# A two-layer trunk: the modulation pieces of FFN two and three computed in the Even mixer, each visit's matmuls in reversed order

## The chip, the cores and the metric

The kernel runs on one core of one Trainium2 chip. Its time is device microseconds of one execution. The core's engines run side by side and wait for each other by semaphores: TensorE (PE; PEld is its weight load), VectorE (DVE), ScalarE (ACT), GpSimd (POOL) and SyncE (SP), which here only issues DMAs. ACT issues some DMAs as well.

## The reference

640 tokens of width 1024 (128 context tokens, 512 latent ones) pass two layers. Each layer is an FFN half step, a token mixer and another FFN half step, each between two RMS norms and each modulated by a condition (one vector for the context tokens, one for the latent ones):

```python
def adaln(cond, w, b):                       # mod_w[i]: 1024 x 9216, one per layer
    m = (silu(cond) @ w + b).reshape(cond.shape[0], 1, 9, D_MODEL)
    return [m[:, :, j] for j in range(9)]    # shift, scale, gate for each of the three sublayers
x = x + 0.5 * gate * rmsnorm(swiglu(rmsnorm(x, g_pre) * (1 + scale) + shift), g_post)   # FFN
x = x + gate * rmsnorm(mixer(rmsnorm(x, g_pre) * (1 + scale) + shift), g_post)          # mixer
```

The mixer of layer 0 ("Even") is a bidirectional gated DeltaNet with four heads beside multi-head latent attention with four heads; that of layer 1 ("Odd") is gated linear attention. The FFN's inner width is 2816. Everything is float32.

The modulation product is the part that the change moves: 2 rows times a 1024 x 9216 matrix, twice, some 75 MB of weights for very little arithmetic.

## The kernel before

There are six sublayers in a row: FFN 1, Even, FFN 2 (layer 0), FFN 3, Odd, FFN 4 (layer 1). Large products are done as three products of float32r halves (`hi`, `lo`): `L650` is an FFN's input product, `L298` every output product, `L208` a mixer's input product. Weights go by SP's queue from HBM into seven buffers of 512 KB (`rawp`, `raw()`), are split by ACT and DVE, and the buffer is free again.

**Modulation.** `adaln` (a generator, L364 and on) works in 80 *pieces*: layer, column group q (five of 2048 columns, the last of 1024) and row block kc (eight of 128 rows). A piece loads two halves of 512 KB (one in the last group) into `raw` buffers. Every second piece there is a *visit*: the matmuls of two pieces, each 128x32 weights (the two conditions, padded to 32) against 128x512 of the matrix; the four of a piece lie at column offsets 0, 32, 64 and 96 of PE and write four stripes of one PSUM bank. A matmul shows as two records in the trace. In the first group each piece is a visit of its own. After the eighth piece of a group its result is added to a bias in one more `raw` buffer (`mb`, L403), and for four of the five groups transposed on PE (L407) in a bank of the pool `ps_pt`, of which there are two; the DVE then copies shift and scale out. Gates go to DRAM.

`filler` does one piece. It is called 8 times at the start, after each of 16 steps of FFN 1's loop and 6 times in its tail, in the mixer through `fill` 31 times (after values and z blocks, between the heads of the attention by the table `MFILL`), 10 times in FFN 2's loop and 6 in its tail, and in FFN 3's loop until nothing is left (3 pieces). `FILLS` holds the counts of FFN 1 to 4. In the mixer `look` is set: a piece's load is issued one call ahead.

**The Even mixer.** Blocks of the input product, a short convolution, then the DeltaNet in two pairs of heads: `gdn_prep`, `gdn_inverse`, `gdn_levels` (two levels with transposes, then a last level of 128x64 matmuls), `gdn_chain` (four steps and one for the context, each a `gdn_step`), with the attention heads `mla_head` between and beside them. The two PSUM banks of `ps_pt` and the two of `ps_dn` serve both pairs for the whole stretch (`banks`), so a modulation transpose finds no bank of `ps_pt` before they are done. At the end come `out_rows` and `finish`, which is also the seam to the next sublayer.

**What sets the order.** A scheduler orders each engine's instructions when the program is built. It walks along in time; whenever an engine is free, it takes the instruction of highest priority among those that are ready by its own estimates (program order, but for those under `ahead`). A modulation matmul that is ready can so be pulled far forward into a hole, and a visit can be cut by other work. Its estimate for a modulation matmul charges the one at column offset 0 with the whole stream of 512 columns and those at other offsets with almost nothing. In the built program, of the matmuls of the mixer from piece 43 on, 19 of 20 at offset 0 are followed by other work, and of those at offsets 32 and 64 two of 40. On the chip each engine then works strictly in that order.

Of the kernel before, what the change touches and what calls it, by code (L numbers as in the profile page):

```python
# [22 lines left out]
KC = 8  # L23
# [4 lines left out]
HW = (6400, 4096)  # L28
HT = TOK // 2
PLAIN = 2  # L30
FILLS = (((16, 6), (10, 6)), ((18, 0), (0, 0)))
EARLY = 5
SLOTS = ((2, 3, 4, 5, 6), (0, 1, 2, 3, 4))
TW = 648
# [47 lines left out]
class Trunk:  # L82
# [281 lines left out]
    def adaln(self, mod_w, mod_b, norm_post):  # L364


        nc = self.nc
        order = iter([(l, q, kc) for l in range(2) for q in range(5) for kc in range(KC)])
        ready = []

        def load():
            for l, q, kc in order:
                wt = []
                for half in range(2 if q < 4 else 1):
                    w = self.W(name="mw") if (l, q) == (0, 0) else self.raw("mw")
                    nc.sync.dma_start(w, mod_w[l, kc * P:(kc + 1) * P, q * 2048 + half * 1024:q * 2048 + half * 1024 + 1024])
                    wt.append(w)
                ready.append(wt)
                return

        for l in range(2):
            for q in range(5):
                nj = 4 if q < 4 else 2
                rows = 32 * nj
                ps = self.ps_ad.tile([P, 512], F32, tag="ad", name=self.u("ad"))
                held = []
                for kc in range(KC):
                    if not ready:
                        load()
                    held.append((kc, ready.pop(0)))  # L390
                    if self.look:
                        load()
                    one = (l, q) == (0, 0)
                    for k, wt, j in [(k, wt, j) for k, wt in held for j in range(nj)] if one or kc % 2 else []:
                        nc.tensor.matmul(ps[32 * j:32 * j + 32, :], lhsT=self.cT[:, k], rhs=wt[j // 2][:, (j % 2) * 512:(j % 2) * 512 + 512], start=k == 0, stop=k == KC - 1, tile_position=(0, 32 * j))
                    if one or kc % 2:
                        held = []
                    if kc < KC - 1:
                        yield False
                mb = self.raw("mb")  # L400
                b = mod_b[l, q * 2048:q * 2048 + 512 * nj]
                nc.scalar.dma_start(mb[0:rows, 0:512], bass.AP(b.tensor, b.offset, [[512, nj], [0, 32], [1, 512]]))
                nc.vector.tensor_add(mb[0:rows, 0:512], mb[0:rows, 0:512], ps[0:rows, :])  # L403
                if q < 4:
                    pt = self.pt()
                    for c4 in range(4):
                        nc.tensor.transpose(pt[:, c4 * P:(c4 + 1) * P], mb[:, c4 * P:(c4 + 1) * P], self.ident)  # L407
                for mi in range(nj // 2):
                    n = 2 * q + mi
                    if n % 3 < 2:  # L410
                        for r in range(2):
                            src = pt.rearrange("p (c m j r) -> p c m j r", c=4, m=2, j=2)[:, :, mi, :, r]
                            nc.vector.tensor_copy(self.modF[l][:, n, r].rearrange("p (j c) -> p c j", c=4), src)
                    else:
                        o = 64 * mi
                        g = norm_post[l, n // 3]
                        nc.scalar.dma_start(mb[o:o + 64, 512:1024], bass.AP(g.tensor, g.offset, [[512, 2], [0, 32], [1, 512]]))
                        nc.vector.scalar_tensor_tensor(mb[o:o + 64, 0:512], mb[o:o + 64, 0:512], 1.0 if n // 3 == 1 else 0.5, mb[o:o + 64, 512:1024], ALU.mult, ALU.mult)
                        for j in range(2):
                            nc.scalar.dma_start(self.gate_dr[l][n // 3][:, j * 512:j * 512 + 512], mb[o + 32 * j:o + 32 * j + 2, 0:512])  # L420
                yield True
# [471 lines left out]
class Even(Mixer):  # L893
# [87 lines left out]
    def run(self, nxt):  # L981
        T, nc, i = self.T, self.T.nc, self.i
# [3 lines left out]
        k, q, vtok, vpad = ([None] * NH for _ in range(4))  # L986
# [179 lines left out]
        def gdn_prep(pair, st, misc, ering):  # L1166
            for c in range(NT):
                cs = slice(c * P, (c + 1) * P)
                pb, pk, E = misc(), misc(), ering()
                for u, d, h in units(pair):  # L1170
                    nc.tensor.transpose(un(pb, u), gc[:, d, c, h:h + 1].to_broadcast([P, P]), T.ident)
                for h2 in range(2):
                    kc = k[2 * pair + h2][:, cs]
                    nc.tensor.matmul(un(pk, 2 * h2), lhsT=kc, rhs=kc, start=True, stop=True)
                    nc.tensor.matmul(un(pk, 2 * h2 + 1), lhsT=kc, rhs=q[2 * pair + h2][:, cs], start=True, stop=True)
                for u, d, h in units(pair):
                    nc.vector.scalar_tensor_tensor(un(E, u), un(pb, u), gc[:, d, c, h:h + 1], neg[d], ALU.subtract, ALU.min)
                nc.scalar.activation(E[:, :512], E[:, :512], AF.Exp)
                pair_view = lambda t, h2: t[:, h2 * 256:h2 * 256 + 256].rearrange("p (d t) -> p d t", d=2)
                if c:  # L1180
                    Qe = st.Q[c]
                    nc.scalar.activation(Qe, pb, AF.Exp)
                    for h2 in range(2):
                        w = pair_view(Qe, h2)
                        nc.vector.tensor_mul(w, w, q[2 * pair + h2][:, cs].unsqueeze(1).to_broadcast([P, 2, P]))
                for h2 in range(2):
                    nc.vector.tensor_mul(pair_view(st.att[c], h2), pair_view(E, h2), un(pk, 2 * h2 + 1).unsqueeze(1).to_broadcast([P, 2, P]))
                for u, d, h in units(pair):
                    nc.vector.scalar_tensor_tensor(un(st.A[c], u), un(pk, 2 * (u // 2)), nbp[:, c, d * 4 + h:d * 4 + h + 1], un(E, u), ALU.mult, ALU.mult)
# [35 lines left out]
        def gdn_levels(st):  # L1225
            for lv in (4, 5):
                mask = T.cm[:, lv].unsqueeze(1).to_broadcast([P, 4, P])
                for c in range(NT):
                    a, uu, dd = st.A[c], st.U[c], st.D[c]
                    py, pz = misc(), misc()  # L1230
                    for u in range(4):
                        nc.tensor.matmul(un(py, u), lhsT=un(a, u), rhs=un(dd, u), start=True, stop=True)
                    Y = ering()
                    nc.scalar.copy(Y[:, :512], py)
                    for u in range(4):
                        nc.tensor.matmul(un(pz, u), lhsT=un(Y, u), rhs=un(uu, u), start=True, stop=True)
                    nc.vector.copy_predicated(v4(uu), mask, v4(pz))
                    for u in range(4):
                        nc.tensor.transpose(un(py, u), un(uu, u), T.ident)
                    nc.scalar.copy(dd, py)  # L1240

            lo, hi = slice(0, 64), slice(64, 128)
            where = ((hi, lo), (lo, hi))
            for c in range(NT):
                a, uu, dd = st.A[c], st.U[c], st.D[c]
                py, pz, Y = misc(), misc(), ering()
                for u in range(4):
                    r, k = where[u % 2]
                    nc.tensor.matmul(un(py, u)[r, k], lhsT=un(a, u)[:, r], rhs=un(dd, u)[:, k], start=True, stop=True, tile_position=(0, r.start))
                by = lambda t, d: t[:, :512].rearrange("p (h d t) -> p h d t", h=2, d=2)[:, :, d]  # L1250
                for d, (r, k) in enumerate(where):
                    nc.scalar.copy(by(Y, d)[r, :, k], by(py, d)[r, :, k])
                for u in range(4):
                    r, k = where[u % 2]
                    nc.tensor.matmul(un(pz, u)[k, r], lhsT=un(Y, u)[:, k], rhs=un(uu, u)[:, r], start=True, stop=True, tile_position=(0, k.start))
                for d, (r, k) in enumerate(where):
                    nc.vector.tensor_copy(by(uu, d)[k, :, r], by(pz, d)[k, :, r])

        def gdn_step(pair, st, work, S, cu, last, ctx):

            at = lambda c: slice(c * P, (c + 1) * P)
            if not last:
                pt, kdt = misc(), work()
# [23 lines left out]
            for u, d, h in units(pair):  # L1287
                c = cu[d]
# [316 lines left out]
        one = (mb, hq, prs, pTs)  # L1605
# [486 lines left out]
```

## Time and profile before

| | |
|---|---|
| median of three runs | 2714.06 us (2709.87 to 2714.55) |
| the profiled execution | 2716.26 us, of it 2714.5 us in the span |
| mean granted clock of PE | 0.991 |
| PE busy | 2632.5 us, 97% |
| PE's weight loads | 2331.2 us, 86% |
| DVE busy | 1943.0 us, 72% |
| ACT busy | 1179.1 us, 43% |
| HBM | 113 GB/s over the span |

"Busy" is time in which at least one instruction of an engine is shown. Matmuls overlap, and their ends are modelled: the end of one can lie behind the start of the next. The granted clock is a share of 2.4 GHz; 0.50 is the lower of its two levels, 1.2 GHz.

### The profile page before, as it was taken

The numbers are of one execution on the slowest core, as the hardware profiler recorded it, in microseconds if no ns is written. First come the engines' busy times: TensorE is split into PE (matmuls) and PEld (weight loads), VectorE is DVE, ScalarE is ACT, GpSimd is POOL, SyncE is SP. The second block draws the span as 40 slices with busy tenths as digits, with TensorE's granted clock in tenths as the row PEclk, the third lists the DMA queues.
The fourth block names the chain that finished last, engine by engine and source line by source line (L and its number), as shares of the span: only waits on it lengthen the run. The fifth ranks groups of instructions, "written<-read, shape, count | busy, mean of one in ns | idle before, by whom it ended". The sixth has DMA issues, their size and how long they took to land. (4 is left out here: it accounts for less than half of the span.)

```text
span 2714.5 us, 41232 instructions
## 1 busy us (share of the span) xinstructions
PE 2632.5 (97%) x16040; PEld 2331.2 (86%) x16040; DVE 1943.0 (72%) x3731; ACT 1179.1 (43%) x2281; POOL 125.5 (5%) x301
## 2 busy tenths in 40 slices
PE   6999999999999999999999999999999999999998
PEld 4988888789858678888997999999899988999997
DVE  5777777768585558777778777777675749777776
ACT  5433333554345645332335433334765447333333
POOL 0000000200100010000001000000200002000001
PEclk8999999999999999999999999999999999999999
DMA  8334424734151334343227322224212143332222
GB/s 272 123 115 141 148 96 133 251 103 142 50 188 46 128 117 130 114 138 103 86 71 244 104 87 86 86 81 135 92 55 67 59 140 109 95 92 86 78 70 101
DMA packets 297099, 309.60 MB, mean 114 GB/s; under 512 B 13573, under 2 KB 250639, under 8 KB 296903
## 3 DMA queue, kind: packets, MB, share of 16 engines
q1 hardware_dynamic: 278240, 260.05, 30.1%
q10 hardware_dynamic: 18663, 46.92, 4.9%
q8 instruction: 126, 2.06, 0.3%
q14 instruction: 70, 0.57, 0.1%
HBM read 286.59 MB, written 20.33 MB: 113 GB/s over the span
## 5 line engine op out<-in xcount | busy, mean ns | idle before, releaser
L650 PE MATMUL up<-ar,hi 128*128 128x320 f32 x2944 | 658.6, 311 | 10.5 <-ACT ar L513 4.5
L650 PEld LDWEIGHTS up<-ar,hi 128*128 128x128 f32 x2944 | 502.4, 189 | 37.2 <-ACT ar L513 6.1
L650 PE MATMUL up<-ar,lo 128*128 128x320 f32 x1472 | 455.5, 310 | 0.6 <-DVE lo L604 0.6
L603 ACT CAST hi<-raw 128x1024 fp32r<-128x1024 f32 x256 | 268.1, 1050 | 295.4 <-PE up L650 258.4
L304 DVE TENSOR_TENSOR y<-y,dn 128x512 f32<-128x512 f32 x388 | 264.5, 682 | 151.9 <-PE dn L298 150.8
L604 DVE TENSOR_TENSOR lo<-raw,hi 128x1024 fp32r<-128x1024 f32 x256 | 312.4, 1222 | 75.1 <-ACT hi L603 74.5
L298 PE MATMUL dn<-hi,al 128*128 128x512 f32 x880 | 347.8, 395 | 0.1
L298 PE MATMUL dn<-lo,ah 128*128 128x512 f32 x880 | 347.6, 395 | 0.0
L298 PE MATMUL dn<-hi,ah 128*128 128x512 f32 x880 | 346.8, 395 | 0.7 <-DVE y L304 0.5
L650 PE MATMUL up<-hq,hi 128*128 128x320 f32 x1408 | 315.1, 310 | 0.3 <-DVE xn L707 0.3
L650 PEld LDWEIGHTS up<-ar,lo 128*128 128x128 f32 x1472 | 277.9, 189 | 1.3 <-DVE lo L604 1.3
L208 PE MATMUL up<-ar,hi 128*128 128x384 f32 (+1 forms) x1184 | 267.3, 315 | 4.9 <-ACT ar L274 4.0
L650 PEld LDWEIGHTS up<-hq,hi 128*128 128x128 f32 x1408 | 238.8, 188 | 21.5 <-issue 9.2
L650 PE MATMUL up<-hq,lo 128*128 128x320 f32 x704 | 217.4, 309 | 0.0
L208 PEld LDWEIGHTS up<-ar,hi 128*128 128x128 f32 x1184 | 200.6, 191 | 15.3 <-issue 5.6
L183 DVE TENSOR_TENSOR lo<-raw,hi 128x1024 fp32r<-128x1024 f32 x145 | 175.8, 1218 | 45.0 <-ACT hi L182 38.2
L298 PEld LDWEIGHTS dn<-hi,al 128*128 128x128 f32 x880 | 165.3, 188 | 39.3 <-DVE al L691 1.2
L298 PEld LDWEIGHTS dn<-hi,ah 128*128 128x128 f32 x880 | 165.2, 188 | 26.3 <-DVE y L304 1.4
L208 PE MATMUL up<-ar,lo 128*128 128x384 f32 (+1 forms) x592 | 184.3, 311 | 0.0
L298 PEld LDWEIGHTS dn<-lo,ah 128*128 128x128 f32 x880 | 165.1, 188 | 22.2
L182 ACT CAST hi<-raw 128x1024 fp32r<-128x1024 f32 x145 | 150.9, 1048 | 44.5 <-PE up L208 19.0
L658 ACT COPY h<-up 128x320 f32<-128x320 f32 x68 | 29.0, 426 | 314.3 <-PE up L650 314.3
(704 smaller groups left out, 4216.2 us busy)
## 6 DMA issues: line engine op xcount, KB each, us to landing
raw<-in_ffn_w_in_dram SPq DMA_DIRECT2D x188, 512.0 KB
mw<-in_mod_w_dram SPq DMA_DIRECT2D x144, 512.0 KB
raw<-in_ffn_w_out_dram SPq DMA_DIRECT2D x88, 512.0 KB
xdr<-x ACTq DMA_DIRECT2D x25, 512.0 KB
x<-xdr ACTq DMA_DIRECT2D x25, 512.0 KB
raw<-in_od_w_in_dram SPq DMA_DIRECT2D x24, 512.0 KB
raw<-in_ev_w_in_dram SPq DMA_DIRECT2D x19, 512.0 KB
gb<-gate ACTq DMA_DIRECT2D x12, 512.0 KB
```

What stands on the lines that cost most here:

```text
L182: nc.scalar.copy(hi, raw)
L183: nc.vector.tensor_sub(lo, raw, hi.bitcast(F32))
L208: self.nc.tensor.matmul(ps[:, :n], lhsT=wt[a][:, kc], rhs=self.h[g][:, b, kc], start=k == 0, stop=k == 3 * KC - 1)
L298: nc.tensor.matmul(ps, lhsT=a(i, m), rhs=w[j][:, nh * 512:nh * 512 + 512], start=k == 0, stop=k == last)
L304: nc.vector.tensor_add(yd, yd, ps)
L603: nc.scalar.copy(hi, raw[:, :n])
L604: nc.vector.tensor_sub(lo, raw[:, :n], hi.bitcast(F32))
L650: nc.tensor.matmul(ps[:, :HT], lhsT=w[i][:, kc], rhs=b[j].at(kc), start=first and n == 0, stop=n == 11, skip_group_check=not first)
L658: self.T.nc.scalar.copy(p1, X[:, :HT])
```

## The change

The counts of FFN 2 and FFN 3 become 0, and the mixer calls `fill` at three more places: before each of the five chunks of `gdn_prep` for the second pair, in two of the five chunks of each of the two levels in `gdn_levels` (called for both pairs), and at the start of every `gdn_step` (five per pair): 5 + 8 + 10 = 23 calls. In a visit the pieces are taken in reversed order, and the four matmuls of a piece from column offset 96 down to 0. `begin` and `end` set the start and stop marks of the accumulation for that order: the first piece that is multiplied starts each stripe, the last one stops it.

```diff
-FILLS = (((16, 6), (10, 6)), ((18, 0), (0, 0)))
+FILLS = (((16, 6), (0, 0)), ((0, 0), (0, 0)))
...
                     one = (l, q) == (0, 0)
-                    for k, wt, j in [(k, wt, j) for k, wt in held for j in range(nj)] if one or kc % 2 else []:
-                        nc.tensor.matmul(ps[32 * j:32 * j + 32, :], lhsT=self.cT[:, k], rhs=wt[j // 2][:, (j % 2) * 512:(j % 2) * 512 + 512], start=k == 0, stop=k == KC - 1, tile_position=(0, 32 * j))
+
+                    for n, (k, wt, j) in enumerate([(k, wt, j) for k, wt in reversed(held) for j in reversed(range(nj))] if one or kc % 2 else []):
+                        begin, end = k == kc and kc == (0 if one else 1), kc == KC - 1 and n >= (len(held) - 1) * nj
+                        nc.tensor.matmul(ps[32 * j:32 * j + 32, :], lhsT=self.cT[:, k], rhs=wt[j // 2][:, (j % 2) * 512:(j % 2) * 512 + 512], start=begin, stop=end, tile_position=(0, 32 * j))
...
                 pb, pk, E = misc(), misc(), ering()
+                if pair:
+                    self.fill(1)
                 for u, d, h in units(pair):
...
                     py, pz = misc(), misc()
+                    if c % 2:
+                        self.fill(1)
                     for u in range(4):
...
         def gdn_step(pair, st, work, S, cu, last, ctx):
 
+            self.fill(1)
             at = lambda c: slice(c * P, (c + 1) * P)
```

## Rows read from the trace of the kernel before

**Rows 1.** The page's first part: engine, busy us, share, instructions.
```profile
PE 2632.5 (97%) x16040; PEld 2331.2 (86%) x16040; DVE 1943.0 (72%) x3731; ACT 1179.1 (43%) x2281; POOL 125.5 (5%) x301
```

**Rows 2.** Windows, all instructions: stretch, length, busy, clock, DMA share, GB/s.
```profile
500.00:530.00 30.00, 28.36 (x154) 17.63 (x152) 19.57 (x38) 17.11 (x42) 7.07 (x23) 1.00 0.72 243
...
690.00:945.00 255.00, 247.93 (x1754) 185.53 (x1753) 164.43 (x591) 126.85 (x359) 13.70 (x18) 0.99 0.31 109
...
1040.00:1440.00 400.00, 399.02 (x2389) 364.77 (x2389) 299.47 (x456) 146.29 (x216) 2.36 (x6) 1.00 0.35 109
1440.00:1500.00 60.00, 57.59 (x317) 44.93 (x316) 53.04 (x116) 37.69 (x98) 9.87 (x24) 0.97 0.61 207
```

**Rows 3.** Waits of PE from 690 to 945: total us, times, longest.
```profile
PE up L1457 <- POOL ro L235: 1.9, 1, 1.9
PE up L1532 <- DVE hq L1501: 0.9, 1, 0.9
```

**Rows 4.** Windows again, two short stretches; the third number from behind is the clock.
```profile
705.00:710.00 5.00, 5.00 (x30) 4.84 (x30) 2.28 (x7) 1.07 (x2) 0.00 (x0) 0.66 0.04 13
1473.00:1476.00 3.00, 3.00 (x10) 0.76 (x8) 3.00 (x10) 0.72 (x2) 0.00 (x0) 0.50 0.67 201
```

**Rows 5.** Timeline of PE, a visit in FFN 2's loop: start, length.
```profile
1112.22 1.92 PE L395 MATMUL ad<-mw,cT 128*32 128x512 f32 x16
1114.08 0.56 PE L650 MATMUL up<-hq,hi 128*128 128x320 f32 x2
```

**Rows 6.** Timeline of PE, three runs of modulation in the mixer.
```profile
738.81 1.07 PE L395 MATMUL ad<-mw,cT 128*32 128x512 f32 x8
...
740.23 1.04 PE L395 MATMUL ad<-mw,cT 128*32 128x512 f32 x2
...
741.85 1.06 PE L395 MATMUL ad<-mw,cT 128*32 128x512 f32 x6
```

**Rows 7.** Windows, line L395 alone: stretch, length, PE, PEld, clock, DMA.
```profile
500.00:530.00 30.00, 9.10 (x48) 1.54 (x48) 1.00 0.72 243
...
690.00:945.00 255.00, 31.49 (x160) 4.55 (x160) 0.99 0.31 109
...
1100.00:1440.00 340.00, 7.69 (x64) 1.67 (x64) 1.00 0.35 112
1440.00:1500.00 60.00, 9.33 (x34) 1.81 (x34) 0.97 0.61 207
1500.00:1600.00 100.00, 3.81 (x14) 0.74 (x14) 1.00 0.36 114
```

**Rows 8.** Timeline of PE, seam of FFN 2 and 3, and a last-group visit.
```profile
1467.60 1.06 PE L395 MATMUL ad<-mw,cT 128*32 128x512 f32 x6
1470.94 0.81 PE L650 MATMUL up<-ar,hi 128*128 128x320 f32 x3 [2.29 <-ACT ar L513]
...
1472.58 5.32 PE L395 MATMUL ad<-mw,cT 128*32 128x512 f32 x16
...
1570.20 1.91 PE L395 MATMUL ad<-mw,cT 128*32 128x512 f32 x8
```

**Rows 9.** Timeline of PE, transposes of two closed groups at the mixer's end.
```profile
948.90 1.05 PE L407 MATMUL pt<-ident,mb 128*128 128x128 f32 x8
```

**Rows 10.** Timeline of PE, first and last of nine runs beside attention heads.
```profile
877.00 1.06 PE L395 MATMUL ad<-mw,cT 128*32 128x512 f32 x8
...
925.99 1.06 PE L395 MATMUL ad<-mw,cT 128*32 128x512 f32 x6
```

**Rows 11.** Timeline of PE, four matmuls of the last inversion level.
```profile
729.96 0.45 PE L1249 MATMUL pt<-g,g 128*64 128x64 f32 x8
```

**Rows 12.** Timeline of PE, tail of FFN 1: first and last of six runs.
```profile
512.09 1.05 PE L395 MATMUL ad<-mw,cT 128*32 128x512 f32 x4
...
524.51 1.05 PE L395 MATMUL ad<-mw,cT 128*32 128x512 f32 x4
```

**Rows 13.** Waits of SP's queue from 690 to 945: total us, times, longest.
```profile
SPq L376 <- PE ad L395: 135.7, 17, 29.0
```

## The prediction

> **What bounds the kernel now.** The page's busy row first [rows 1]: TensorE (PE) is busy 97% of the span, DVE 72%, and nothing else is near. Then the stretches [rows 2]: in the second FFN's loop (1040 to 1440 us) PE is busy 399.02 of 400 us, in the Even mixer's second part (690 to 945) 247.93 of 255, at the seam of the second and third FFN (1440 to 1500) 57.59 of 60. So a PE microsecond taken out of an FFN loop is a microsecond of the kernel, and one put into the mixer costs nearly one. The reader is to see that there is little idle time to hide work in: 255 - 247.93 = 7.07 us in the mixer's second part, the largest piece a wait of 1.9 us for a POOL power [rows 3], which also leaves PE at a granted clock of 0.66 over the next 5 us [rows 4], another 0.34 x 5 = 1.7 us.
>
> What a visit costs depends on how it is cut. In an FFN loop one visit (two pieces, 8 matmuls, 16 records) is one run: it starts at 1112.22 and the next instruction at 1114.08, so 1.86 us of PE, of 1.92 us shown, since each run laps 0.06 us into what follows [rows 5]. In the mixer the same visit comes as runs of 2, 8 and 6 records that take 1.04, 1.07 and 1.06 us [rows 6]: a run of one matmul costs as much as one of four, because matmuls of different column groups stream together and the passes of one matmul follow each other. The runs break after the matmul at column offset 0, so the first matmul of a piece is torn from the other three. Modulation alone, by stretch [rows 7]: 160 records, ten visits, take 31.49 us in the mixer's second part, in 29 runs (counted in the timeline); less 29 x 0.06 this is 29.7 us, 2.97 per visit instead of 1.86.
>
> **The change, part by part.** *Removed from the second and third FFN:* nine visits, 7.69 + 9.33 + 3.81 = 20.83 us [rows 7], in ten runs, so 20.2 us of PE. Two things of this don't come back. The run of 6 at 1467.60 ends in a wait for ScalarE's cast, until 1470.94 [rows 8]; without it PE waits there anyway: 1.06 off. And the 16 records at 1472.58 take 5.32 us, while 8 of the same kind take 1.91 [rows 8]: the granted clock is 0.50 just there [rows 4], since PE had stood idle. The idle time stays, so the slow clock will hit other matmuls: 5.32 - 2 x 1.91 = 1.5 off. Net -17.7 us. Bounds: -20.2 if both come back; -11 if the seam is held by its chain through DVE and ACT (DVE 53.04 of 60 [rows 2]) and gives back the rest of its 9.33, 6.8 us. I take -17.7: PE's own idle time there is 2.41 of 60 us, so it is the nearer bound.
>
> *Moved, not removed:* the four transposes that close a group of pieces and the DVE copies behind them. In the mixer the two GDN pairs hold both transpose banks, so the transposes of two groups wait until 948.90 and run there as 8 in 1.05 us [rows 9]; in future four groups do. Nothing in the sum. The loads move with the pieces: 10 pieces of two halves and 8 of one, 28 transfers of 512 KB, leave SP's queue in the FFNs, whose loop has PE busy through, and join it in the mixer; what they may do there is rival 2.
>
> *Added to the mixer:* fill calls: 5 in the second pair's preparation, 4 in each of two level stages, 5 in each of two chains, 23 in all; 19 are needed, the last 4 of the mixer's calls find nothing left. So the calls for pieces 62 to 80 join those for 43 to 61 there. Visit 62 is pulled forward into the mixer already; its second part gets 19 visits, 44 to 80, instead of 10.
>
> *The reversed order.* The scheduler's estimate charges the matmul at column offset 0 for the whole stream and the other three almost nothing; so whatever became ready meanwhile goes in right behind offset 0. Reversed, offset 0 is the last of each piece, and the break falls between whole pieces: two runs of 8, each 1.06 - 0.06 = 1.00 us [rows 6, 10]. That descending offsets stream together as well is seen in the last inversion level, whose offsets alternate 64, 0, 64, 0: 8 records in 0.45 us [rows 11]. So 19 x 2.00 = 38.0 us in place of 29.7: +8.3. Bounds: whole visits 19 x 1.86 = 35.3, +5.6; order without effect 19 x 2.97 = 56.4, +26.7.
>
> *The tail of the first FFN* issues three visits as 24 records and six runs of 4, at 512.09 the first and 524.51 the last [rows 12], broken where a half of a piece landed: 9.10 us [rows 7] less 7 x 0.06 = 8.7. Reversed, each visit waits for its last half and then runs whole: 1.86 + 2 x 2.00 = 5.9, -2.8. Bounds 0 and -3.1. PE is busy 28.36 of 30 us there [rows 2], so I take it in full. The first visits, at the kernel's start, wait on landing and norms; 0.
>
> *Idle time in the mixer.* Between -8.8 (all 7.07 idle and 1.7 of clock filled) and +9 (the nine runs from 877.00 to 925.99 [rows 10] now fill holes of the attention heads; if the pieces are used up before, about 1.00 us opens for each). I take 0, because the pieces are late rather than early: SP's modulation loads waited 135.7 us in 17 waits for the matmuls to free the raw buffers [rows 13], and they will still come in until the mixer's end.
>
> Sum: -17.7 + 8.3 - 2.8 + 0 = -12.2 us. The profiled run took 2716.26 us (span 2714.5); it gives 2704.1. The median of the runs shown is 2714.06, 2.2 below it: 2701.9, said as 2702.
>
> A rule weighed: PE's weight loads fill 185.53 of the 255 us in the mixer's second part and 364.77 of 400 in the FFN loop [rows 2]. The Trainium skill (Perfetto Trace Analysis, section Identifying the Most-Contended Engine) says that a busy PE row is a poor measure of how full PE is, and that the share of weight loads and the useful operations are to be judged by instead; by that the mixer has a quarter of its time to spare and the sum would be that of rival 1. The trace agrees only in part: the modulation runs have weight loads in 4.55 of their 31.49 us [rows 7] and still hold PE all the time.
>
> **Rivals.**
> 1. *Hidden in the mixer* (the share of weight loads taken as headroom): the 19 visits fit into PE time that looks busy and isn't, and cost no more than ten did. For it: weight loads at 73% there. Against: runs follow each other without a gap, and the listed waits are short [rows 3]. -17.7 - 2.8 = -20.5: 2693.5.
> 2. *Held back by buffers.* Seven raw buffers carry all weights. Each closed group keeps one until its transposes get a bank: now two, until 948.90 [rows 9]; then four. A visit needs four buffers landed before its first matmul, and with the four left after the third closed group none can be loaded ahead, so visits arrive late, holes open early and SP's output weights queue behind. For it: SP's waits [rows 13]. Against: PE's longest waits in the mixer are for POOL and DVE, not for a landing [rows 3]. Idle +9 instead of 0: -3, 2711.
> 3. *Slower: the cut stays.* If other work becomes ready at each matmul whatever the order, visits keep 2.97 us and the tail its runs: -17.7 + 26.7 = +9.0, 2723. It decides from (17.7 + 29.7) / 19 = 2.49 us per visit upward. For it: more visits stand among short chain operations. Against: breaks come after offset 0 and hardly elsewhere.
>
> That the change doesn't do what it says needs no rival of its own: the calls suffice for all 80 pieces, and a late piece is rival 2.
>
> **Chances.** Forecast 0.47 (own range 2694 to 2709), rival 1 0.13, rival 2 0.25, rival 3 0.15. What this kernel's measurement tells from no change is about 0.2%, 5.4 us: 2708.6 to 2719.5. Faster: 0.43 of the forecast, 0.13, and 0.02 of rival 2: 0.58. Same: 0.04 of the forecast, 0.23 of rival 2 and 0.01 of rival 3, 0.28. Slower: 0.14. Range 2690 to 2719: it leaves out most of rival 3 (0.14) and an edge of rival 1 (0.04).
>
> **What would show it.** No modulation matmul after about 1040 us, and an FFN loop of the second FFN shorter by 4 x 1.86 = 7.4 us. In the mixer runs of 8 and 16 records, hardly any of 2 or 6, and modulation's busy time in its second part near 40 us. The tail of the first FFN with modulation near 6 us instead of 9.10. The mixer's end later by about 8 us against its start. Wrong would be: runs of 2 and 6 as before, PE waits for modulation landings, or the mixer later by more than 18 us.

## The result, and the profile after

The changed kernel takes 2734.62 us (median; 2733.34 to 2735.85) against 2714.31 us: a ratio of 1.0079, with a 95% interval of 1.0061 to 1.0096. It is slower by 20 us, where 12 us faster was forecast. The page's first part of the changed kernel: engine, busy us, share, instructions. It answers to [rows 1].

```profile
PE 2625.5 (96%) x16040; PEld 2332.2 (85%) x16040; DVE 1939.3 (71%) x3731; ACT 1183.3 (43%) x2283; POOL 129.2 (5%) x301
```

PE is busy 7 us less than before in a span 18.3 us longer, so about 25 us of idle time have appeared over the whole span. To find where, the span is cut at the first matmul of each sublayer's first product, and the mixer also where its last input product ends and its first output product begins ("second part"; before 693.89 to 948.35, after 695.68 to 984.96):

| stretch | before | after | difference |
|---|---|---|---|
| start, to FFN 1's first product | 44.43 | 50.40 | +6.0 |
| FFN 1 | 465.78 | 460.22 | -5.6 |
| mixer, input products | 183.69 | 185.06 | +1.4 |
| mixer, second part | 254.46 | 289.28 | **+34.8** |
| output product of the mixer, FFN 2 and FFN 3 | 973.28 | 953.85 | -19.4 |
| Odd and FFN 4 | 792.9 | 794.0 | +1.1 |

The sum is +18.3, the difference of the spans. The FFNs give back what was forecast (-17.7) and 1.7 us more; nearly all of the loss stands in one stretch. Windows of the changed kernel, all instructions: stretch, length, busy of PE, PEld, DVE, ACT and POOL, clock, DMA share, GB/s. The first two answer to [rows 2], the third is the mixer's second part.

```profile
500.00:530.00 30.00, 25.15 (x159) 18.26 (x159) 21.23 (x40) 17.91 (x44) 7.82 (x26) 1.00 0.72 246
...
1078.00:1478.00 400.00, 399.08 (x2369) 371.20 (x2368) 303.43 (x469) 154.28 (x234) 2.72 (x8) 1.00 0.31 92
...
695.68:984.96 289.28, 269.74 (x1867) 189.89 (x1865) 164.72 (x593) 130.46 (x367) 10.82 (x13) 0.95 0.45 148
```

Windows of the changed kernel, the modulation's line L397 alone (PE, PEld, clock, DMA), to set beside [rows 7]:

```profile
505.00:530.00 25.00, 5.77 (x48) 1.25 (x48) 1.00 0.81 274
...
695.68:984.96 289.28, 45.85 (x272) 6.66 (x272) 0.95 0.45 148
1000.00:2732.00 1732.00, 0.00 (x0) 0.00 (x0) 0.99 0.30 92
```

The same windows of the kernel before, over its own second part: first all instructions, then L395 alone.

```profile
693.89:948.35 254.46, 247.39 (x1755) 184.86 (x1753) 163.84 (x589) 129.03 (x367) 10.77 (x13) 0.99 0.31 109
```

```profile
693.89:948.35 254.46, 31.49 (x160) 4.55 (x160) 0.99 0.31 109
```

These rows split the stretch into three: idle (length less PE busy), modulation, and all other PE work. Before it is 7.07 + 31.49 + 215.90, after 19.54 + 45.85 + 223.89. So +12.5 is idle, +14.4 modulation, and +8.0 is other work that has become slower, though it is the same 1595 records (1755 - 160, 1867 - 272): the mean clock is 0.95 instead of 0.99. What the idle time waits for, PE in the changed kernel's second part (total us, times, longest), to set beside [rows 3]:

```profile
PE ad L397 <- DMA mw<-in_mod_w_dram: 4.9, 3, 4.5
PE pt L1245 <- DVE ar L1243: 4.5, 1, 4.5
PE pt L1361 <- DVE kq L1321: 2.7, 2, 1.8
PE up L1553 <- ACT cq L1578: 2.0, 1, 2.0
```

The longest of the first line (4.5 us) is a visit that waits for its weights, the second an inversion level that waits for DVE. DVE's timeline there shows why:

```profile
871.30 0.69 DVE L405 TENSOR_TENSOR mb<-mb,ad 128x512 f32<-128x512 f32 x1 [8.63 <-DMA mb<-in_mod_b_dram]
871.91 0.72 DVE L1243 COPY_PREDICATED ar<-cm,dn 128x512 f32<-128x512 uint8 x1
```

The bias add of a closed group stands 8.63 us for its bias, and the level's copy, which comes behind it on DVE, holds PE. After each of the four longest waits the clock is down. Windows of the changed kernel behind them, at 780 (1.8 us), 822, 868 and 915 us (the third number from behind is the clock):

```profile
781.00:785.00 4.00, 4.00 (x20) 2.09 (x24) 3.99 (x15) 1.03 (x3) 0.00 (x0) 0.57 0.36 88
826.00:832.00 6.00, 5.29 (x23) 2.05 (x24) 5.41 (x30) 1.59 (x5) 0.00 (x0) 0.50 0.43 124
870.00:877.00 7.00, 4.32 (x20) 3.49 (x22) 2.06 (x4) 1.07 (x2) 0.00 (x0) 0.51 0.22 75
918.00:925.00 7.00, 6.08 (x18) 1.98 (x17) 3.44 (x10) 2.03 (x5) 0.82 (x1) 0.52 0.49 154
```

At 826.71 a whole visit, 16 records, takes 3.64 us there; in an FFN loop it took 1.92 [rows 5]. The visits themselves are cut as forecast: 37 runs, 25 of them of 8 records, two of 16, eight of 4 (the last group's half-size pieces), one each of 2 and 6. Their busy time is 45.85 us, where near 40 was said. Two of the prediction's signs of being wrong are there: PE waits for a modulation landing, and the second part is longer by 34.8 us, more than 18.

### The profile page after: what moved, and what is told of

It reads as the page before. It is cut to its first block, busy times and chain, and to the rows that moved or that the text cites. A ratio compares the mean times of both kernels' runs of the same rounds, so it can differ in the third digit from the quotient of the medians.

```text
span 2732.8 us, 41267 instructions
## 1 busy us (share of the span) xinstructions
PE 2625.5 (96%) x16040; PEld 2332.2 (85%) x16040; DVE 1939.3 (71%) x3731; ACT 1183.3 (43%) x2283; POOL 129.2 (5%) x301
## 5 line engine op out<-in xcount | busy, mean ns | idle before, releaser
L652 PEld LDWEIGHTS up<-hq,hi 128*128 128x128 f32 x1408 | 239.0, 188 | 18.3 <-issue 6.7
```

Of the source, the lines that this page charges most:

```text
L652: nc.tensor.matmul(ps[:, :HT], lhsT=w[i][:, kc], rhs=b[j].at(kc), start=first and n == 0, stop=n == 11, skip_group_check=not first)
```

## The experiments

All ratios are to the kernel before on the same chip. One table carries their second part of the mixer, split as above (us, from the windows of each run); the rows on which a verdict rests follow in their places. "Torn" visits have the matmul order of before, "whole" ones the reversed order. The ratios come from several executions of each kernel, the other columns from one traced execution. Single executions of one kernel differ by 1 to 19 us (`pt_ad` by most, 2722.03 to 2740.74), so a few us between two rows are not resolved. Each kernel also has the rest of its program laid out anew by the scheduler, and no run holds that order fixed.

| kernel | visits there | length | idle | modulation | other PE work | clock | ratio |
|---|---|---|---|---|---|---|---|
| before | 10 torn | 254.46 | 7.07 | 31.49 | 215.90 | 0.99 | 1 |
| order_only | 10 whole | 254.60 | 8.54 | 25.69 | 220.37 | 0.97 | 1.0027 |
| no_mod | none | 257.52 | 20.85 | 0 | 236.67 | 0.90 | 0.9948 |
| before_no_loads | 11 torn, no loads | 256.92 | 6.92 | 31.37 | 218.63 | 0.97 | 1.0003 |
| changed | 19 whole | 289.28 | 19.54 | 45.85 | 223.89 | 0.95 | 1.0079 |
| fills_only | 19 torn | 291.31 | 9.90 | 62.73 | 218.68 | 0.99 | 1.0093 |
| no_loads | 19 whole, no loads | 273.69 | 7.48 | 41.47 | 224.74 | 0.96 | 1.0005 |
| torn_no_loads | 19 torn, no loads | 272.18 | 3.67 | 52.08 | 216.43 | 0.99 | 1.0009 |
| half_loads | 19 whole | 286.18 | 17.69 | 47.23 | 221.26 | 0.95 | 1.0074 |
| thin_loads | 19 whole | 289.76 | 20.56 | 46.32 | 222.88 | 0.96 | 1.0094 |
| bias_own | 19 whole | 286.97 | 17.99 | 46.31 | 222.67 | 0.96 | 1.0053 |
| pt_ad | 19 whole | 290.09 | 16.27 | 45.78 | 228.04 | 0.96 | 1.0058 |
| both_ad | 19 whole | 292.36 | 15.98 | 46.12 | 230.26 | 0.94 | 1.0039 |
| late_sites | 14 whole | 270.70 | 12.89 | 38.44 | 219.37 | 0.96 | 1.0061 |
| early_sites | 17 whole | 282.08 | 20.19 | 40.10 | 221.79 | 0.96 | 1.0072 |
| no_prep_fill | 19 whole | 286.53 | 21.95 | 43.61 | 220.97 | 0.97 | 1.0078 |

**The two halves of the change, each alone.** `order_only` takes the reversed order and keeps the old calls; `fills_only` the reverse.

```diff
 # order_only: the changed kernel with
-FILLS = (((16, 6), (0, 0)), ((0, 0), (0, 0)))
+FILLS = (((16, 6), (10, 6)), ((18, 0), (0, 0)))
-                if pair:
-                    self.fill(1)
...
 # fills_only: the changed kernel with the loop over matmuls, its start and stop marks of before
```

> Only the reversed order; fills as in the kernel before. Theory A (the order mends the cut, the fills do the harm): the ten visits of the mixer's second part cost 10 x 2.00 instead of 29.7 us, -9.7; the start is 6.0 later and FFN 1 5.6 shorter as in the changed kernel, +0.4: about 2705 us. Theory B (the order itself brings the idle time, since a visit then waits for its last half): the mixer gains nothing or gets longer, 2714 to 2725 us.

> Only the moved fills; matmuls in the order of before. Removal of the nine visits from FFN 2 and 3 -19.4 us as measured in the changed kernel. Theory A: 19 visits x 2.97 instead of 29.7 us, +26.7, and the idle and slow clock of the changed kernel's mixer, +26: about 2747 us. Theory B: the idle time comes with the order, so without it -19.4 + 26.7: about 2721 us.

Measured: 2720.85 us (1.0027, 1.0018 to 1.0037) and 2739.68 us (1.0093, 1.0080 to 1.0106). The order alone comes out in theory B's range, the fills alone between the two. Theory B's reason is not seen, though: none of PE's waits in `order_only`'s second part is for a landing. The order takes 5.8 us of modulation out of the mixer's second part and the stretch stays as long: 254.60 against 254.46. All instructions of `order_only` there, beside the row of before above:

```profile
695.71:950.31 254.60, 246.06 (x1765) 186.89 (x1763) 163.38 (x589) 129.70 (x367) 10.77 (x13) 0.97 0.33 110
```

The gain goes into idle time (+1.5) and a slower clock (other work +4.5). Its timeline shows such a place among the attention heads, with no run in it:

```profile
885.52 0.33 PE L1586 MATMUL up<-ident,pr 128*128 128x128 f32 x1 [0.93 <-ACT pr L1582]
886.20 0.66 PE L1570 MATMUL up<-ident,pr 128*128 128x128 f32 x4 [0.36 <-ACT ob L1587]
887.10 0.47 PE L1577 MATMUL up<-ident,pr 128*128 128x128 f32 x1 [0.24 <-ACT pr L1558]
888.25 0.69 PE L1356 MATMUL pt<-ident,kq 128*128 128x128 f32 x2 [0.67 <-DVE kq L1316]
...
889.53 2.33 PE L1581 MATMUL up<-V,pT 128*128 128x128 f32 x10
```

Four waits add up to 2.2 us, and over the 5 us from 888 the granted clock is 0.50.

**No modulation, and modulation without loads.** In `no_mod` the second layer's pieces do nothing but the bias; in `no_loads`, `before_no_loads` and `torn_no_loads` their matmuls stay and read one still tile.

```diff
 # no_mod and the three without loads
-                for half in range(2 if q < 4 else 1):
+                for half in range(0 if l else 2 if q < 4 else 1):
...                   (no_mod also leaves out layer 2's matmuls and the add of their sum)
 # no_loads; the same in the kernel before and in fills_only
-  rhs=wt[j // 2][:, (j % 2) * 512:(j % 2) * 512 + 512]
+  rhs=self.still if l else wt[j // 2][:, (j % 2) * 512:(j % 2) * 512 + 512]
```

> The changed kernel without loads and matmuls of the second layer's modulation (only the bias is left of it). Shows what the mixer's second part takes with no modulation in it. If visits cost their own time and no more in the kernel before, it is 254.5 - 29.6 = 225 us with idle time near 7 us, and the kernel is about 2671 us. If ten visits filled holes that now open, it is 235 to 245 us with 15 us or more of idle time and half-clock stretches, and the kernel 2680 to 2691 us.

> The changed kernel with all matmuls of the second layer's modulation (pieces 41 to 80) kept, but on one still tile in place of the loaded weights: their loads, raw buffers and landing waits are left out. Theory T (the idle time and the slow clock of the mixer's second part come from the transfers: landings, raw buffers, bias loads behind them in the queues): that part shrinks from 289.3 to 263 us, which is 254.5 + 8.4 of modulation as forecast, and the kernel to about 2708 us. Theory P (they come from the order: 38 runs of 1 us put between short steps of chains, whatever is loaded): it stays at 283 to 289 us, the kernel at 2729 to 2735 us.

> The kernel before (ten torn visits in the mixer's second part) with the second layer's modulation matmuls on a still tile: their loads, raw buffers and landing waits are left out. Theory T (in the changed kernel loads cost the mixer 15.6 us because four groups and 28 more transfers meet there; with the ten visits of before they cost little): its second part stays at 250 to 255 us, of 254.5. Theory U (each load costs the mixer, whoever moves it): 10 of 19 visits' share of 15.6, so 246 us.

> Moved fills in the order of before (19 torn visits) with the second layer's modulation matmuls on a still tile, loads left out. With loads the mixer's second part took 291.3 us, with whole runs and no loads 273.7. Theory T (loads add their 15.6 us whatever the order): 276 us. Theory V (torn visits have enough slack between them to hide the landings: idle time is 2.8 us above that of before, no more): 286 to 291 us.

Measured: 2701.15 us (0.9948, 0.9934 to 0.9963), 2716.93 (1.0005, 0.9995 to 1.0015), 2714.02 (1.0003, 0.9994 to 1.0012) and 2715.81 (1.0009, 1.0000 to 1.0018). The row of `no_mod` surprises most:

```profile
692.48:950.00 257.52, 236.67 (x1595) 195.28 (x1593) 161.97 (x588) 129.20 (x367) 10.86 (x13) 0.90 0.09 30
```

Without any modulation the stretch is 3 us longer than with ten visits, outside both figures expected. The 31.49 us taken out come back as 13.8 us of idle time and 20.8 us of slower other work, at a mean clock of 0.90. Its longest waits of PE there:

```profile
PE up L1554 <- ACT hq L1508: 3.4, 1, 3.4
PE dn L1246 <- DVE g L1244: 3.3, 1, 3.3
PE up L1592 <- ACT pr L1588: 3.2, 4, 2.0
```

So the ten visits of before were free, as far as one trace of each kernel tells: without them the same stretch is no shorter, and what stands in their place is waits of the mixer's own chains and a lower clock. It also fits that making them shorter brought nothing. That the rest of the program is laid out anew in `no_mod` is a rival that no run excludes; the second pair's preparation at least ends where it did (51 us into the stretch, before 50). Visits beyond the ten are not free. Without loads 19 visits take 273.69 us whole and 272.18 torn:

```profile
694.15:967.84 273.69, 266.21 (x1866) 192.15 (x1865) 165.20 (x593) 130.17 (x367) 10.79 (x13) 0.96 0.09 29
```

```profile
692.05:964.23 272.18, 268.51 (x1866) 188.96 (x1865) 165.56 (x593) 130.57 (x367) 10.77 (x13) 0.99 0.09 29
```

Torn or whole is the same again: 10.6 us less modulation against 3.8 us more idle time and 8.3 us of slower other work. Nine visits more cost 273.69 - 254.60 = 19.1 us whole and 272.18 - 254.46 = 17.7 torn, about 2.0 each, near their own time. The loads come on top: 289.28 - 273.69 = 15.6 us whole (theory T had 26, theory P none to 6), 19.1 torn (theory T, not V); beside the visits of before they cost nothing (256.92 without, 254.46 with; 2 us above theory T's range, far from U's 246).

**Which part of the loads.** `bias_own` loads the bias into a buffer of its own; `pt_ad` makes the closing transposes in the accumulation bank, so a closed group frees its raw buffer at once; `both_ad` does both. `half_loads` halves bytes and buffers, `thin_loads` the bytes alone.

```diff
 # bias_own
+                bi = self.bip.tile([P, 512], F32, tag="bi", name=self.u("bi"))
...
-                nc.scalar.dma_start(mb[0:rows, 0:512], ...)
+                nc.scalar.dma_start(bi[0:rows, :], ...)
...
 # pt_ad
-                    pt = self.pt()
+                    pt = self.ps_ad.tile([P, 512], F32, tag="ad", name=self.u("pt"))
 # half_loads
+                for half in range(2 if q < 4 and not l else 1):
...
+  rhs=wt[0 if l else j // 2][...]
 # thin_loads
+                    m = 512 if l else 1024        # columns loaded of each half
...
```

> The changed kernel with the bias of a closed group loaded into a buffer of its own (512 columns), not into the raw buffer of the result; so its load needs no free raw buffer and can lie early. Theory A1 (DVE stands at the bias add until the bias lands, 16.9 us in three waits, and the inversion levels behind it hold PE): the 4.5 us wait of PE at 868 us goes with the 6.8 us of half clock behind it (3.4 us), about -8 of 2734.6: 2727 us. Theory A2 (the raw buffers held by closed groups are the cause, the bias only one sign): -0 to -3, 2732 to 2735 us.

> The changed kernel with the four transposes that close a group in the accumulation bank of the modulation instead of a bank of ps_pt; so they need not wait for the mixer's end, and a closed group gives its raw buffer back at once. Theory A2 (four closed groups hold four of seven raw buffers until 985 us, weights land late, PE and DVE wait): the landing wait of 4.5 us at 822 us and the bias waits go with the slow clock behind them, -8 to -16: 2718 to 2727 us. Theory A1 (the bias load is late for itself, whatever the buffers): at most -3, since the next group's first matmul now waits for the copies out of the bank.

> The changed kernel with both: the bias in a buffer of its own, and the closing transposes in the accumulation bank. If the two mend different waits, their gains add, -6.6 and -6.4 us from 2734.6: about 2721.5 us. If what they mend is one thing, 2727 to 2728 us as each alone.

> The changed kernel; in the second layer each piece loads only its first half and multiplies both column pairs from it: all matmuls stay, half the bytes and half the raw buffers. With all loads the mixer's second part took 289.3 us, with none 273.7. Theory R (raw buffers: seven carry everything, a visit needs four): 273 to 278 us, the kernel about 2718 us. Theory S (the bytes on the way): the same here. Theory N (neither; the placing of the runs by the scheduler): 285 us or more.

> The changed kernel; in the second layer each half loads only its first 512 columns and multiplies them twice: all matmuls and all raw buffers stay, half the bytes. Theory R: the buffers are held as long, only the landing is sooner, so the second part stays at 284 to 289 us, the kernel at 2729 us or more. Theory S: 273 to 280 us, as with half the loads, the kernel 2718 to 2725 us.

Measured: 2728.03 us (1.0053, 1.0041 to 1.0065), 2728.19 (1.0058, 1.0041 to 1.0076), 2724.01 (1.0039, 1.0027 to 1.0051), 2731.28 (1.0074, 1.0059 to 1.0089) and 2738.11 (1.0094, 1.0077 to 1.0111). The first three are 0.2 to 0.4% below the changed kernel. `bias_own` comes out 1 us from theory A1's 2727, `pt_ad` 1 us above theory A2's range, and `both_ad` between its two figures, 10.6 us below the changed kernel's 2734.62, so the two gains add in part. Where they lie the traces don't show: the second parts take 286.97, 290.09 and 292.36 us (the last two hold closing transposes that stood behind the stretch, 25 records more), and the traced executions of `pt_ad` and `both_ad`, at 2732.87 and 2731.33 us, lie 4.7 and 7.3 us above their medians. The 4.5 us wait at 868 is gone in `bias_own`, and others have come; of its gain in the profiled run, 4.6 us of span, 2.8 us lie in FFN 1. Half the bytes and half the buffers change little (286.18), half the bytes alone nothing (289.76): as theory N said. PE's longest waits in the second part of `half_loads`:

```profile
PE pt L1278 <- DMA g<-in_state_gdn_dram: 3.9, 1, 3.9
PE ad L397 <- DVE nm L1559: 3.3, 1, 3.3
PE up L1586 <- DVE pT L1583: 2.6, 1, 2.6
PE pt L1361 <- DVE kq L1321: 2.6, 2, 1.8
```

No wait for a modulation landing is among the longest, and the idle time is 17.69 us all the same. But the longest is again for a landing, of the DeltaNet's state on ACT's queue; in `pt_ad` and `both_ad` too it is the longest wait, one row of each:

```profile
PE pt L1278 <- DMA g<-in_state_gdn_dram: 4.0, 1, 4.0
```

```profile
PE pt L1280 <- DMA g<-in_state_gdn_dram: 3.6, 1, 3.6
```

In the changed kernel the two waits on transfers (4.5 for weights, 4.5 behind the bias) and the half clock behind them (0.50 over 6 us and 0.51 over 7, by estimate 3.0 and 3.4 us lost) add up to 9.0 + 6.4 = 15.4 us, about the price of the loads. In `half_loads` neither stands among the longest, and the stretch is 3 us shorter. So single waits change hands. Bytes and the number of raw buffers don't set the sum; whether late landings do is not shown.

**The place of the calls.** In every kernel above with 19 visits, loads or not, the transposes of the second pair's preparation end 81 us or more after the second part begins, before at 50. Is it where the visits stand?

```diff
 # early_sites: levels of pair 0, chain of pair 0, preparation of pair 1 (14 calls)
+                    if c % 2 and st is st0:
+            if pair == 0:
 # late_sites: levels and chain of pair 1 (9 calls); no_prep_fill: all but the preparation (18)
+                    if c % 2 and st is not st0:
+            if pair == 1:
 # all three: FILLS as before
```

> The changed kernel with the new calls of the first pair's stages and of the second pair's preparation alone (4 + 5 + 5, all ahead of the second pair's inverse); the counts of FFN 2 and 3 as before, so what is left runs there. In the kernel before, the transposes of that preparation end 50 us after the mixer's second part begins, in the changed kernel 82 us, and the second part without any modulation takes 257.5 us. Theory K (the mixer is held by a chain, and visits ahead of the second pair's preparation put that chain off): it ends at 75 to 90 us again, the second part takes 275 to 290 us, the kernel 2725 to 2735 us. Theory L (each visit costs the same wherever it stands): 14 of 19 pieces, 254.5 + 14/19 x 34.8 = 280 us, but with the preparation's end near 50.

> The changed kernel with the new calls of the second pair's levels and chain alone (4 + 5); counts of FFN 2 and 3 as before. Theory K: the second pair's preparation ends at 50 us as before, the nine pieces take their own PE time at most, the second part 254 to 264 us; FFN 2 and 3 lose five visits; the kernel 2708 to 2716 us. Theory L: 9 of 19 pieces, 254.5 + 9/19 x 34.8 = 271 us, the kernel 2722 us or more.

> The changed kernel without the five calls in the second pair's preparation, 18 new calls left; the last piece goes to FFN 3, counts as before. If the calls inside the preparation put it off: it ends near 50 us, the second part takes 255 to 266 us, the kernel about 2712 us. If those of the first pair's levels and chain do it too: 70 to 90 us, 280 us or more, 2728 us.

Measured: 2733.33 us (1.0072, 1.0055 to 1.0089), 2730.80 (1.0061, 1.0049 to 1.0074) and 2734.64 (1.0078, 1.0062 to 1.0093). The preparation ends at 83, 50 and 76 us, yet theory K falls with `late_sites`: its chain starts as before and the second part still takes 270.70 us, as theory L said (271).

```profile
697.32:968.02 270.70, 257.81 (x1812) 187.20 (x1811) 162.60 (x588) 127.14 (x360) 10.77 (x13) 0.96 0.40 133
```

By visits beyond ten the price is nearly even: +16.2 us for 4, +27.6 for 7, +34.8 for 9 in the changed kernel and +32.1 for 9 in `no_prep_fill`, so 3.6 to 4.1 each with loads. The place moves a chain, the number costs.

**The smaller terms, and a candidate.** `first_fwd` takes the very first group in ascending order; `rev_ffn1` is the kernel before with the reversed order in FFN 1 alone; `best` adds to that `bias_own` and gives the six pieces of FFN 2's tail to FFN 3.

```diff
 # rev_ffn1, in adaln
+                    rev = l == 0 and not one and not self.look
 # best, besides
+FILLS = (((16, 6), (10, 0)), ((18, 0), (0, 0)))
```

> The changed kernel with the column offsets of the very first group of pieces ascending again. If the 6.0 us by which FFN 1 starts later are the price of the order there (a visit needs its second half first), it starts at 44.4 us again; the 5.5 us that FFN 1 gave back show by their own whether they go with it: 2729 us if they stay, 2734 us if FFN 1 gets its half-clock stretches back.

> The kernel before with the reversed order in the loop and the tail of FFN 1 alone; the first group, the mixer, FFN 2 and FFN 3 as before. If whole visits save what the prediction's step on the tail says, FFN 1 is 2.8 us shorter and the rest as before: 2711.5 us. If the tail is held by landings or by the seam's chain instead, no change: 2714 us.

> A candidate: the kernel before with the reversed order in FFN 1 alone (-2.8), the bias in a buffer of its own (FFN 1 was 2.8 us shorter by it), and the six pieces of FFN 2's tail given to FFN 3's loop, where there is room for 18 and three are used (three visits at 1.86 instead of 9.33 us of modulation at the seam, with its half clock: -4). In all -9.6: 2704 us. If the seam is held by DVE and ACT and not by PE, the last part brings nothing: 2708 us.

Measured: 2734.66 us (1.0074, 1.0061 to 1.0087), 2715.13 (1.0010, 1.0001 to 1.0019) and 2713.37 (1.0003, 0.9994 to 1.0012). In `first_fwd` FFN 1 starts 0.9 us later than before instead of 6.0, and 2.6 of the 5.6 us gained in FFN 1 go with it; the total is that of the changed kernel. In `rev_ffn1` FFN 1 is 3.3 us shorter, and the mixer's input products, which follow, are 2.9 us longer: the rows of before and of `rev_ffn1`.

```profile
510.21:693.89 183.68, 179.86 (x1198) 158.00 (x1195) 132.90 (x359) 91.64 (x183) 16.83 (x64) 1.00 0.45 151
```

```profile
506.88:693.45 186.57, 179.71 (x1206) 161.06 (x1203) 133.59 (x361) 91.73 (x183) 17.57 (x66) 0.98 0.45 149
```

`best` misses both its figures: it is 6.1 us ahead when the mixer begins and no faster at the end. No version beats the kernel before.

## Why the prediction was wrong

**Removal from FFN 2 and 3: right.** -17.7 forecast, -19.4 measured. FFN 2's loop, first to last block, went from 316.19 to 306.56 us, 9.6 less where the visits alone made 7.4; the seam, FFN 3 and what else lies in the stretch gave 9.8 of the 10.3 forecast. What made the 2.2 us in the loop is not shown. No modulation stands after 1000 us.

**The step that failed is the price of modulation in the mixer, +8.3, with "Idle time in the mixer", 0.** The mixer's second part grew by 34.8 us. Taken apart along the runs:

| part | forecast | measured | from |
|---|---|---|---|
| the ten visits become whole runs | 20.0 - 29.7 = -9.7 | +0.1 | order_only less before |
| nine visits more, without their loads | 9 x 2.00 = +18.0 | +19.1 | no_loads less order_only |
| their loads | 0 (-8.8 to +9) | +15.6 | changed less no_loads |

The middle term came out about a microsecond off, in part by luck: modulation's busy time grew by 15.8 us (41.47 - 25.69), and 4.4 us of slower other work less 1.1 of idle time made up the rest. The first fell with the sentence "one put into the mixer costs nearly one": it holds for a visit added, but not for time taken out of those that were there. "PE is busy 247.93 of 255" [rows 2] was true, and 31.49 us of it were cover for waits, by `no_mod`: without them PE idles 20.85 us and runs at a clock of 0.90. A busy share does not say what the engine would do if the work were gone. The bound on the clock's side was open only downward (1.7 us to gain); that idle time there is paid twice, once as itself and once as slower matmuls behind it, had no term, though [rows 4] showed it for 705 us.

The third term was bounded at +9 by nine runs that would leave holes. What came instead is waits scattered over the stretch, on a landing, the bias, POOL's power, ACT, the longer of them followed by slow clock. How the loads make them stays open. It is not the bytes or the number of buffers (`thin_loads`, `half_loads`); late landings, the bias's and those held up by closed groups among them, carry a part that the runs don't separate. The scheduler also lays out all engines anew by its own estimates when loads are there to be planned; whether this order or the transfers make the waits no run tells.

**The reversed order did what was said of it.** Runs of 8 instead of 2 and 6; it is only worth nothing in the mixer. Torn runs leave the clock at 0.99 in three kernels of four (0.97 in `before_no_loads`) and whole runs at 0.94 to 0.97, with ten visits and with 19.

**The tail of FFN 1** has 5.77 us of modulation, as forecast (5.9, before 9.10). But `rev_ffn1` shows the -2.8 given back in the stretch behind it, so the term was worth about 0: what ended sooner waited there (idle time in the input products of `rev_ffn1` 6.86 us, before 3.82).

**The rivals.** Rival 1 (hidden) fails: the nine visits without loads cost about their own time. The sum by the Trainium skill's rule (Perfetto Trace Analysis, section Identifying the Most-Contended Engine) fails with it, where weight loads at 73% were read as headroom. Rival 2 named waits by loads and was right that they come. Its mechanism, buffers held by closed groups, was taken away by `pt_ad`: the median fell by 6.4 us, so it is at most a part of the 20, and in the trace the stretch stayed. Rival 3's time, 2723, is the nearest, by another cause: the cut did not stay.

## What to carry to other kernels

Before work is moved into a stage that looks full, take out the work that already fills it, as `no_mod` did: one run hints whether its time is a cost or only cover, and an average per visit tells neither that nor what the next visit costs. Here the first ten visits were free, by that run, and each further one cost about 4 us, twice its own time. Count idle time on TensorE with the clock behind it.

## What the runs showed of the hardware

The clock fell behind quite small waits: behind 1.8 and 0.4 us at 780 us in the changed kernel (0.57 over the next 4 us), behind four of 0.24 to 0.93 us in `order_only` (0.50 over 5 us). The Trainium skill (TensorE: Matmul & The Clock Gate, section "HAM oscillation — how this bites in real kernels") tells of the same loop of waits and slow restarts, with DMA waits of about 3 to 5 us; the trace agrees in kind, with shorter waits. The clock also stays down while PE is shown busy without a break. Windows of `no_loads` from 928, behind its last visit, and of `torn_no_loads` among the same attention heads:

```profile
928.00:946.00 18.00, 17.94 (x53) 12.82 (x53) 6.86 (x27) 6.98 (x22) 0.00 (x0) 0.53 0.18 59
```

```profile
924.00:942.00 18.00, 18.00 (x80) 12.13 (x79) 14.27 (x40) 12.50 (x29) 0.00 (x0) 1.00 0.13 36
```

Both are busy all through; one does 53 matmul records in 18 us at a clock of 0.53, the other 80 at 1.00. The counts are a rough scale, since the second window begins with some 6 us of other products. A busy PE row hides the clock entirely.
